# A two-layer hybrid network on one core: recurrent output projection as Strassen products that begin on sums already in PSUM, and a later start of the inner products in the second MLP

## The chip, the core and the metric

The kernel runs on one core of a Trainium2 chip. The metric is the device time of one execution in microseconds (us), from the first to the last instruction and what the device spends around them. Three runs of the kernel before gave 2066.32, 2066.69 and 2067.29 us; their median, 2066.69 us, is the time before.

## The reference

The sequence has 1024 tokens of 1024 features. There are two layers. Layer 0 mixes with sliding-window attention, layer 1 with a gated linear recurrence of eight heads; each is followed by an MLP with a squared ReLU and 4096 hidden features. All is fp32.

```python
def hgrn2_recurrence(h, lower_bound, w_in, g_norm, w_o):
    q, f, i, g = jnp.split(h @ w_in, 4, axis=-1)
    ...
    o = o.transpose(1, 0, 3, 2, 4).reshape(bsz, seq, HGRN_HEADS * HGRN_DV)
    o = rmsnorm(o, g_norm) * jax.nn.silu(g.astype(jnp.float32))
    return o.astype(h.dtype) @ w_o

def sqrelu_mlp(h, w_up, w_down):
    return jnp.square(jax.nn.relu(h @ w_up)) @ w_down

def reference(x, ...):
    for layer in range(DEPTH):
        h = rmsnorm(x, mix_norm[layer])
        y = sliding_window_attention(h, ...) if layer == 0 else hgrn2_recurrence(h, ...)
        x = x + y
        h = rmsnorm(x, mlp_norm[layer])
        x = x + sqrelu_mlp(h, mlp_w_up[layer], mlp_w_down[layer])
    return rmsnorm(x, final_norm)
```

The change touches the last line of `hgrn2_recurrence` (a product of 1024 x 1024 by 1024 x 1024, the "output projection" here), both MLPs, and the order at the very start.

## The kernel before

Every fp32 product is made of three TensorE products: both operands are split into a high and a low part (`split`, `weight_split`: one ScalarE cast, one VectorE subtraction for each 128x512 tile), and `mm3` adds high x high, high x low and low x high into one PSUM bank. A bank holds 128x512. There are eight: four with the tag `p`, four with the tag `q`.

Activations stand with features in partitions and are cut into two halves of 512 tokens, `hf` 0 and 1. A block product of two halves of features by two halves of tokens is done by Strassen's method in Winograd's form with seven products instead of eight. The products are numbered 1 to 7; 1, 6, 7, 4 share one running sum and 5, 3 (and 2) the others. Product 2 needs the upper features of half 0, product 1 the lower features of half 0, product 5, 6, 7, 3 need half 1, and product 4 needs all.

- **MLP, first projection** (`pair`, 16 pairs of output tiles a layer). Of each pair, products 1, 5, 6 and 7 are plain. From pair 2 on (`leaves`), products 2, 3 and 4 of two pairs together are done by a second, inner Strassen step (`inner_products`): 42 matmuls of 256 columns take the place of 24 matmuls of 512. Products 1 and 2 of pairs 0 and 1 are done ahead (`pair_first`), since they need only half 0.
- **MLP, second projection** (`down`). Passes over 16 contraction tiles: 1 with 5, then 6, 7, 2, 4, 3. Results of a pass are copied out of PSUM, added on VectorE to the others of their quarter, multiplied by the token scale (`scaled_sum`) and added to the residual.
- **Recurrent layer** (`hgrn`): eight heads, `gates` (four input projections) interleaved with `recurrence` of the head before. The gated outputs of each head are split and parked in DRAM (`put_by`), taken back at the end (`take_back`), and `hgrn_out` runs for half 0 and then half 1 as plain products: 8 output tiles x 8 contraction tiles x 3 = 192 matmuls a half. Between the halves `mlp_first` prepares the operands of half 0 for the MLP.
- **Start**: `scaled` splits the normalised input and then calls `token_rstd`, whose matmuls against a 128x1 column sum the squares over features. That matmul needs `sum_squares`, a chain of VectorE additions over all eight input tiles.

The order on every engine is set by the program itself: `Schedule.order` lists the operations with given durations, runs a list scheduler forward, ranks all but TensorE by latest start, and issues the best of four passes. A rank is the place of creation less `lead`. All tiles are recorded at one line, L429, so the rows of the trace are told apart by tile names: `p`, `q` banks; `wh`, `wl` high and low weights; `wr` raw weights; `a`, `t` activations; `m` short-lived sums; `d` DRAM.

Of the kernel before, what the change touches and what calls it, by code (L numbers as in the profile page):

```python
# [17 lines left out]
P = 128  # L18
# [125 lines left out]
FULL = {512: 227.3, 256: 119.8}  # L144
LEAD = 100
WARM = 11
ROWS = 16
EVACUATE = 100
HK = KT // 2


# [223 lines left out]
class Net:  # L375
# [203 lines left out]
    def spread(self, y, n=TH, r=None):  # L579

        r = (r or self.psum("q"))[:, :n]
        for j in range(n // P):
            self.mm(r[:, j * P : j * P + P], y[:, j : j + 1].to_broadcast([P, P]), self.ident, True, True, P, 4)
        return r
# [96 lines left out]
    def mlp_first(self, layer):  # L681
        self.layer, self.hid, self.y = layer, {}, {}
        yield from self.begin(2 + layer)
        self.weigh(0)

    def mlp_second(self):
        self.first = [self.pair_first(m) for m in range(2)]
        x = self.finish(2 + self.layer, keep=True)
        self.weigh(1)
        return x  # L690
# [128 lines left out]
    def pair(self, m, x, leaves):  # L819
# [6 lines left out]
        last, odd = m == half - 1, m % 2  # L826
        inner, four = [], ("12", "56", "73", "4")
        if leaves and odd:
            inner.append((2, (up[m - 1][:, TH:], 2), four, (1, 3, 5, 7)))
# [6 lines left out]
        w = self.strassen_weights(up[m], up[m + half], (2, 3, 4) if leaves else (1, 2), inner)  # L836

# [8 lines left out]
        def between(k):  # L846
            for z in now[k]:
                next(z)

        main, side = self.psum("q") if leaves else self.first[m], self.psum("q")  # L850
        now = [()] * 4
        if leaves:
            self.product(main, w[1], x[1], True)
            u1 = read(main)
            self.sums[2].append((m, u1))
            if odd:
                z2 = leaf(2, ((1, 2), (6, 5), (7, 3), (4,)))
                now = [[z2], [z2], [z2], [z2]]
            elif m > 3:
                z4, z3 = leaf(4, ((1, 2), (6, 5), (7, 3), (4,))), self.rest  # L860
                z3.send(w)
                now = [[z4, z3], [z4, z3], [z4], [z4]]
        between(0)
        self.product(side, w[5], x[5], True)
# [34 lines left out]
        if odd:  # L899
            for n, u in self.sums[2][-2:]:  # L900
                self.square_relu(n, 0, u, False)
        elif m > 3:
# [68 lines left out]
    def down(self, cut):  # L971
# [9 lines left out]
        def products(names, ps, ws, start, stop, tokens=slice(0, TH), ms=range(HK)):  # L981
            for p in ps:
                for name in names:
                    (wh, wl), (xh, xl) = ws[name, p]
                    for m in ms:
                        out = (main if name in (1, 6, 7, 4) else side)[m][:, tokens]
                        c = slice(m * P, m * P + P)
                        more = {"skip_group_check": True} if name in (6, 7, 4) or not start else {}
                        first = p == 0 and not more
# [468 lines left out]
    def recurrence(self, e, gates, totals, out):  # L1458
# [80 lines left out]
        for hf, (q, k) in enumerate(zip(qs, ks)):  # L1539
# [34 lines left out]
            self.stt(g, o, self.gain(5, e), g, ALU.mult, ALU.mult)  # L1574
            keep = e < KT - 1
# [30 lines left out]

    def hgrn_out(self, hf, y, total):
        r = self.t()
        self.copy(r, self.rstd(total, 0.25, 0.25))
        for m in range(KT):  # L1610
            w = self.blocks(self.weight(self.io["wg"][m]))
            x = self.t()
            self.dma(x, self.x[m][hf], 4 * P * TH)
            ps = self.psum()
            for kt in range(KT):
                self.mm3(ps, w[kt], y[kt], kt == 0, kt == KT - 1)
            z = self.t()
            self.tt("DVE", z, ps, r, ALU.mult)
            self.x[m][hf] = self.a()
            self.tt("any", self.x[m][hf], x, z, ALU.add)  # L1620

# [9 lines left out]
    def hgrn(self, layer):  # L1631
# [6 lines left out]
        self.spill(1)  # L1638
        ys, totals = [[], []], []
        before = iter(())  # L1640
        for e in range(KT):
            got = []
            interleave(self.gates(e, x, self.rs, r, got, [None] * 2 if e else begun), before, 14, 13)
            before = self.recurrence(e, got, totals, ys)
        run(before)
        for y in ys:
            y[:-1] = [self.take_back(kept) for kept in y[:-1]]
# [53 lines left out]
def layout(i):  # L1701
# [22 lines left out]
        "win": f(win.reshape(KT, P, 4, KT, P).transpose(2, 3, 1, 0, 4).reshape(4, KT, P, D)),  # L1724
        "wg": f(i["hgrn_w_o"][0].reshape(KT, P, KT, P).transpose(2, 1, 0, 3).reshape(KT, P, D)),
        "up": f(i["mlp_w_up"].reshape(2, KT, P, MT, P).transpose(0, 3, 2, 1, 4).reshape(2, MT, P, KT * P)),
# [39 lines left out]
```

## Time and profile before

| | us |
|---|---|
| median of three runs | 2066.69 |
| the profiled execution, its own time | 2068.61 |
| its span, first to last instruction | 2066.8 |
| TensorE busy | 2057.5 |
| VectorE busy | 1831.0 |
| ScalarE busy | 1203.6 |

The profiled execution took 1.8 us more than its span and 1.9 us more than the median of the runs without a profile. "Busy" of TensorE is the union of pipelined matmuls, each longer than the distance to the next, so its rate is read from the start of one stretch to the start of the next rather than from durations. By stage: attention up to about 300 us, its MLP to about 955, the recurrence to about 1366, its output projection to 1446, the second MLP to the end.

### The profile page before, as it was taken

The page shows a single profiled execution, that of the slowest core. Times are in us where ns is not written, and L with a number is a line of the kernel's source. Part 1 is how long each engine was busy: PE and PEld are TensorE (multiplying, and loading weights), DVE is VectorE, ACT ScalarE, POOL GpSimd, SP SyncE. Part 2 cuts the span into 40 slices and gives each one's busy share as a digit, 9 for nine tenths or more (in the row PEclk, how much of TensorE's full clock was granted, in tenths as well). Part 3 has the DMA queues.
Part 4 walks back from the last instruction along what each step waited for, and adds up shares of the span by engine and source line. Part 5 has one row for each costly group of instructions (what it writes and reads, how often), then busy time and mean ns, then how long its engine had stood idle before and what let it go on. Part 6 is the DMA issues. An engine that isn't in the chain of part 4 may idle for free.

```text
span 2066.8 us, 35765 instructions
## 1 busy us (share of the span) xinstructions
PE 2057.5 (100%) x12248; PEld 1747.5 (85%) x12248; DVE 1831.0 (89%) x3696; ACT 1203.6 (58%) x2468; POOL 54.7 (3%) x121
## 2 busy tenths in 40 slices
PE   9999999999999999999999999999999999999998
PEld 7878788898898888888888888888888888888888
DVE  8899889999899979889988888887999989986985
ACT  7577887644565444666555555555765456544473
POOL 3020000000000000000000000000000000000000
PEclk9999999999999999999999999999999999999999
DMA  6212477877679977541322222677887768986822
GB/s 220 82 49 80 128 237 257 278 244 237 225 253 304 332 222 257 196 138 67 113 102 95 96 103 103 219 239 226 273 275 256 230 229 265 311 315 210 270 67 82
DMA packets 225750, 407.43 MB, mean 197 GB/s; under 512 B 25232, under 2 KB 30352, under 8 KB 225568
## 3 DMA queue, kind: packets, MB, share of 16 engines
q1 hardware_dynamic: 225536, 405.12, 59.3%
q8 instruction: 96, 1.57, 0.3%
q14 instruction: 86, 0.70, 0.1%
q10 hardware_dynamic: 32, 0.03, 0.0%
HBM read 321.17 MB, written 83.89 MB: 196 GB/s over the span
## 4 chain that ended last, share of the span: by engine, by line
PE 96%; issue 1%; DVE 1%; ACT 0%; DMA 0%; POOL 0%; POOLq 0%; SPq 0%; DVEq 0%; ACTq 0%
PE p L429 51%; PE q L429 45%; DVE a L429 1%; DMA a<-in_x 0%; DVE m L429 0%; DVE t L429 0%; DVE wl L429 0%; ACT t L429 0%; ACT a L429 0%; DVE sm L429 0%; ACT wh L429 0%; POOL a L429 0%; POOLq L1740 0%; SPq L429 0%; ACT m L429 0%
## 5 line engine op out<-in xcount | busy, mean ns | idle before, releaser
L429 PE MATMUL p<-a,wh 128*128 128x512 f32 (+1 forms) x2880 | 805.0, 364 | 0.0
L429 PE MATMUL q<-a,wh 128*128 128x512 f32 x2112 | 652.9, 390 | 0.0
L429 PEld LDWEIGHTS p<-a,wh 128*128 128x128 f32 x2880 | 515.2, 189 | 84.4 <-issue 0.4
L429 PE MATMUL p<-a,wl 128*128 128x512 f32 (+1 forms) x1440 | 520.5, 362 | 0.0
L429 PEld LDWEIGHTS q<-a,wh 128*128 128x128 f32 x2112 | 389.7, 188 | 75.5
L429 PE MATMUL q<-a,wl 128*128 128x512 f32 x1056 | 410.2, 389 | 0.0
L429 ACT CAST wh<-m 128x512 fp32r<-128x512 f32 (+1 forms) x338 | 206.3, 613 | 262.1 <-PE q L429 172.2
L429 ACT CAST wh<-wr 128x512 fp32r<-128x512 f32 (+1 forms) x351 | 210.9, 603 | 227.8 <-PE p L429 165.2
L429 PEld LDWEIGHTS p<-a,wl 128*128 128x128 f32 x1440 | 271.6, 189 | 40.3 <-DVE wl L429 0.2
L429 DVE TENSOR_TENSOR wl<-m,wh 128x512 fp32r<-128x512 f32 (+1 forms) x338 | 226.8, 676 | 52.1 <-ACT wh L429 47.4
L429 DVE TENSOR_TENSOR wl<-wr,wh 128x512 fp32r<-128x512 f32 x352 | 233.2, 666 | 35.6 <-ACT wh L429 34.6
L429 PEld LDWEIGHTS q<-a,wl 128*128 128x128 f32 x1056 | 198.3, 188 | 41.9
L429 DVE TENSOR_TENSOR a<-t,a 128x512 fp32r<-128x512 f32 (+2 forms) x314 | 207.1, 679 | 14.5 <-PE q L429 8.8
L429 DVE TENSOR_TENSOR t<-t,t 128x512 f32<-128x512 f32 (+3 forms) x337 | 196.7, 602 | 13.8 <-ACT t L429 8.2
L429 ACT CAST a<-t 128x512 fp32r<-128x512 f32 (+1 forms) x234 | 139.1, 610 | 31.7 <-DMA t<-d 10.5
L429 ACT ACTIVATE t<-t 128x512 f32<-128x512 f32 x180 | 113.3, 632 | 73.4 <-DVE t L429 70.3
L429 ACT COPY t<-q 128x512 f32<-128x512 f32 (+2 forms) x201 | 111.3, 558 | 28.8 <-PE q L429 23.3
L429 PE MATMUL p<-wh,a 128*128 128x512 f32 x384 | 125.7, 397 | 0.0
L429 DVE TENSOR_TENSOR m<-wr,wr 128x512 f32<-128x512 f32 (+1 forms) x188 | 121.6, 647 | 2.9 <-DMA wr<-in_down 1.6
L429 DVE TENSOR_TENSOR t<-t,p 128x256 f32<-128x256 f32 x294 | 119.7, 416 | 3.7 <-PE p L429 1.8
L429 PEld LDWEIGHTS q<-t,t 128*64 128x64 f32 (+1 forms) x2160 | 96.0, 144 | 12.1 <-issue 8.1
L429 PE MATMUL q<-t,t 128*64 128x32 f32 (+2 forms) x2160 | 104.7, 229 | 0.0
(129 smaller groups left out, 2327.4 us busy)
## 6 DMA issues: line engine op xcount, KB each, us to landing
t<-d SPq DMA_DIRECT2D x548, 256.0 KB, 4.2
d<-t SPq DMA_DIRECT2D x244, 256.0 KB, 3.2
wr<-in_down SPq DMA_DIRECT2D x224, 256.0 KB, 4.2
wr<-in_up SPq DMA_DIRECT2D x178, 256.0 KB, 3.8
wr<-in_win SPq DMA_DIRECT2D x68, 256.0 KB, 2.8
a<-d SPq DMA_DIRECT2D x60, 256.0 KB, 3.7
wr<-in_wqkv SPq DMA_DIRECT2D x48, 256.0 KB, 2.9
d<-a SPq DMA_DIRECT2D x48, 256.0 KB, 3.9
```

Source lines behind the costliest of these rows:

```text
L429: fn(*[place(a) for a in args], **{k: place(v) for k, v in kw.items()})
```

## The change

1. The output projection becomes seven Strassen products (`hgrn_out`, in the order 1, 5, 2, 6, 3, 7, 4). `recurrence` no longer splits the gated output as it is, but hands it to `out_operands`, which forms the differences that the seven products need and parks them in DRAM. `out_weight` forms the sums of weights, from another layout of the weights in DRAM.
2. Product 2 has its own banks (`side`, tag `q`). So that it adds onto product 1, a matmul first writes each of these banks (its result is not used), ScalarE copies product 1's sum over it, and product 2 accumulates. Products 3 and 4 begin in the same way on sums that ScalarE or VectorE wrote into `side`.
3. `hgrn_out` is now one generator: after product 2 and after product 4 it yields, and four steps of `mlp_first` follow.
4. In the second MLP, inner products start at pair 4 instead of pair 2 (`INNER = 2, 4`); pairs 2 and 3 are done with all seven plain products. The token sums of squares (`weigh`) of that layer move behind pair 1.
5. In both second projections, two quarters are copied into `side` ahead of passes 2 and 3, which then accumulate onto them; the additions afterwards go away.
6. At the start, `token_rstd` of half 0 gets a later rank (`BEHIND`).

```diff
+BEHIND = 120
+INNER = 2, 4
+FIRSTS = 2, 2
+ORDER, AHEAD, HELD = (1, 5, 2, 6, 3, 7, 4), 2, (3, 7, 4)
...
     def scaled(self, which, hf):
-        return h, self.token_rstd(self.sum_squares([self.x[kt][hf] for kt in range(KT)]))
+        total = self.sum_squares([self.x[kt][hf] for kt in range(KT)])
+        self.s.lead = 0 if hf else -BEHIND
+        r = self.token_rstd(total)
+        self.s.lead = 0
+        return h, r
...
     def pair(self, m, x, leaves):
-        elif leaves and m > 3:
+        elif leaves and m > INNER[self.layer] + 1:
...
+        elif not begun:
+            own = self.psum()
+            self.product(main, w[1], x[1], True)
+            u1 = read(main)
+            self.product(own, w[2], x[2], True)
+            self.tt("DVE", u1, own, u1, ALU.add)
+            self.square_relu(m, 0, u1, False)
...
     def mlp(self, cut):
-            if m == 2:
+            if m == INNER[self.layer]:
...
-            self.pair(m, x, m > 1)
+            self.pair(m, x, m >= INNER[self.layer])
+            if self.layer and m == 1:
+                self.weigh(0)
+                self.weigh(1)
...
     def down(self, cut):
-        for i in range(2):
-            for m in range(HK):
-                z = residual(m + (1 - i) * HK, 1)
-                scaled_sum(1, z, y[1 - i, 1, m])
-                self.x[m + (1 - i) * HK][1] = z
+        for m in range(HK):
+            z = residual(m + HK, 1)
+            scaled_sum(1, z, y[1, 1, m])
+            self.x[m + HK][1] = z
+        for m in range(HK):
+            self.copy(side[m], y[0, 0, m], psum=False)
         run_pass((2,))
-        parts = [self.t() for _ in range(HK)]
         for m in range(HK):
-            self.copy(parts[m], side[m])
+            z = residual(m, 0)
+            scaled_sum(0, z, side[m])
+            self.x[m][0] = z
         for m in range(HK):
-            self.tt("DVE", y[0, 0, m], parts[m], y[0, 0, m], ALU.add)
-            z = residual(m, 0)
-            scaled_sum(0, z, y[0, 0, m])
-            self.x[m][0] = z
+            self.copy(side[m], y[0, 1, m], psum=False)
+            self.x[m][1] = residual(m, 1)
         run_pass((4,))
...
     def recurrence(self, e, gates, totals, out):
-            y = self.split(g, self.t if keep else None)
-            out[hf].append(self.put_by(y) if keep else y)
+            self.out_operands(e, hf, g, out)
...
+    def out_operands(self, e, hf, g, x):
+        def put(name, z):
+            y = self.split(z, self.a if last else self.t)
+            x[name].append(y if last else self.put_by(y))
+        if hf == 0:
+            put(1 if e < HK else 2, g)
+            self.beside = g
+        elif e < HK:
+            self.tt("any", self.beside, g, self.beside, ALU.subtract)
+            put(5, self.beside)
+            self.later.append((self.keep(self.beside), self.keep(g)))
+        else:
+            t, q = (self.back(z) for z in self.later[p])
+            self.tt("any", t, g, t, ALU.subtract)
+            put(6, t)
...
+    def hgrn_out(self, x, totals):
...
+        products(1, main, True)
+        for m in range(HK):
+            self.copy(p1[m], main[m])
+        products(5, main, False)
+        for m in range(HK):
+            w, z = ready[2, 0]
+            self.mm(side[m], w[0][:, :P], z[0], True, True)
+            self.copy(side[m], p1[m], psum=False)
+            self.tt("DVE", p5[m], main[m], p1[m], ALU.subtract)
+        products(2, side, False)
+        for m in range(HK):
+            scaled_sum(0, m, side[m])
+        yield
+        products(6, main, False)
+        for m in range(HK):
+            self.copy(side[m], main[m])
+        products(3, side, False)
+        for m in range(HK):
+            scaled_sum(1, m, side[m])
+        products(7, main, False)
+        for m in range(HK):
+            self.tt("DVE", side[m], main[m], p5[m], ALU.subtract)
+            scaled_sum(1, m + HK, main[m])
+        products(4, side, False)
+        for m in range(HK):
+            scaled_sum(0, m + HK, side[m])
+        yield
...
     def hgrn(self, layer):
-        self.hgrn_out(0, ys[0], totals[0])
-        run(self.mlp_first(layer))
-        self.hgrn_out(1, ys[1], totals[1])
+        first = self.mlp_first(layer)
+        for _ in self.hgrn_out(y, totals):
+            for _ in range(HK):
+                next(first)
+        run(first)
```

Here `products(name, bank, start)` runs the 4 x 4 x 3 matmuls of one product, and takes operands back two steps ahead.

How the instructions move is shown at three places. The first is TensorE at the start, in the first of three column groups of the query, key and value projection; `q_400` (before) and `q_466` (the change) are the banks of the sums of squares, `t_234` the sum, `wh` and `wl` the weights of one contraction tile. Before:

```order
L429 MATMUL p_263<-wl_310,a_300 128x512
L429 MATMUL p_263<-wh_294,a_319 128x512
L429 MATMUL p_272<-wh_294,a_300 128x512
L429 MATMUL q_400<-c_69,t_234 128x1 x4
L429 MATMUL p_272<-wl_310,a_300 128x512
L429 MATMUL p_272<-wh_294,a_319 128x512
```

With the change:

```order
L433 MATMUL p_253<-wl_360,a_353 128x512
L433 MATMUL q_466<-c_69,t_234 128x1
L433 MATMUL p_253<-wh_339,a_382 128x512
L433 MATMUL q_466<-c_69,t_234 128x1
L433 MATMUL p_263<-wh_339,a_353 128x512
L433 MATMUL q_466<-c_69,t_234 128x1
L433 MATMUL p_263<-wl_360,a_353 128x512
L433 MATMUL q_466<-c_69,t_234 128x1
```

The four column matmuls stood together behind the 46th matmul of 512 columns, in the fourth contraction tile; now they stand one by one behind the 65th and later, in the sixth.

The second place is TensorE in the output projection, where product 5 ends (`p_16317` is the last of its four banks) and product 2 begins on `q_16893`, `q_16897`, `q_16899`, `q_16902`:

```order
L433 MATMUL p_16317<-a_16263,wl_16593 128x512
L433 MATMUL q_16893<-a_16492,wh_16450 128x512
L433 MATMUL q_16897<-a_16492,wh_16450 128x512
L433 MATMUL q_16899<-a_16492,wh_16450 128x512
L433 MATMUL q_16902<-a_16492,wh_16450 128x512
L433 MATMUL p_16277<-a_16509,wh_16891 128x512
L433 MATMUL p_16277<-a_16518,wh_16891 128x512
L433 MATMUL q_16893<-a_16492,wh_16450 128x512
L433 MATMUL q_16893<-a_16529,wh_16450 128x512
```

The four matmuls that only mark the banks come right behind product 5; two matmuls of product 6 (`p_16277`) stand between them and the first that accumulates. ScalarE has the four copies in one row after the cast of product 6's weight:

```order
L433 CAST wh_16891<-a_16182 128x512
L433 COPY q_16893<-a_16462 128x512
L433 COPY q_16897<-a_16522 128x512
L433 COPY q_16899<-a_16544 128x512
L433 COPY q_16902<-a_16549 128x512
L433 CAST a_16923<-a_16192 128x512
```

Nothing of this stood in the program before. The third place is TensorE where product 4, the last, ends on `q_16902` and the MLP's `pair_first` begins (`q_17489` product 1 of pair 0, `p_17522` its product 2, `q_17527` product 1 of pair 1):

```order
L433 MATMUL q_16902<-a_17008,a_17253 128x512
L433 MATMUL q_16902<-a_17079,a_17253 128x512
L433 MATMUL q_16902<-a_17008,a_17282 128x512
L433 MATMUL q_17489<-a_17057,wh_17023 128x512
L433 MATMUL q_17489<-a_17088,wh_17023 128x512
L433 MATMUL q_17489<-a_17057,wl_17032 128x512
```

After seven more rows of `q_17489`:

```order
L433 MATMUL q_17489<-a_17138,wh_17023 128x512
L433 MATMUL q_17489<-a_17105,wl_17032 128x512
L433 MATMUL p_17522<-a_17511,wh_17044 128x512
L433 MATMUL q_17527<-a_17057,wh_17120 128x512
L433 MATMUL q_17527<-a_17088,wh_17120 128x512
```

Before, the whole of half 0's operands was ready when the projection of half 1 ended. Now `a_17511`, the first operand of product 2, comes from product 4's banks, and twelve matmuls on `q_17489` stand between.

More of the change, by code (lines that the diff above doesn't have):

```diff
@@ L1605, in double @@
         return at + n, new, *out
[L1607 to L1620, printed above, removed]
+    def out_operands(self, e, hf, g, x):
+        p, last = e % HK, e == KT - 1
+        def put(name, z):
[12 more added lines that the diff above has]
+            put(6, t)
+            self.tt("any", self.beside, self.beside, t, ALU.subtract)
+            put(4, self.beside)
+            self.tt("any", q, g, q, ALU.subtract)
+            put(7, q)
+            put(3, g)
@@ new lines, in hgrn_out, with operand, products, scaled_sum @@
+    def hgrn_out(self, x, totals):
+        kept, y, r = {}, {}, [self.a() for _ in range(NH)]
+        order = [(name, p) for name in ORDER for p in range(HK)]
+        ready = {}
+        def operand(name, p):
+            w = self.out_weight(name, p, kept)
+            z = x[name][p]
+            return w, self.take_back(z) if isinstance(z, list) else z
+        def products(name, bank, start, apart=False):
+            todo = order.index((name, 0))
+            for p in range(HK):
+                for q in order[: todo + p + 1 + AHEAD]:
+                    if q not in ready:
+                        ready[q] = operand(*q)
+            got = [ready[name, p] for p in range(HK)]
+            turns = [(p, m) for p in range(HK) for m in range(HK)]
+            more = {} if start else {"skip_group_check": True}
+            for p, m in sorted(turns, key=lambda k: k[1]) if apart else turns:
+                c, (w, z) = slice(m * P, m * P + P), got[p]
+                self.mm3(bank[m], (w[0][:, c], w[1][:, c]), z, start and p == 0, p == HK - 1, **more)
+        def scaled_sum(hf, m, z):
+            u, out = self.t(tag="m"), self.a()
+            self.tt("DVE", u, z, r[hf], ALU.mult)
+            self.dma(out, self.x[m][hf], 4 * P * TH)
+            self.tt("any", out, u, out, ALU.add)
+            self.x[m][hf] = out
+        for hf in range(NH):
+            self.copy(r[hf], self.rstd(totals[hf], 0.25, 0.25))
+        main, side = [self.psum() for _ in range(HK)], [self.psum("q") for _ in range(HK)]
+        p1, p5 = ([self.a() for _ in range(HK)] for _ in range(2))
+        products(1, main, True)
[25 more added lines that the diff above has]
+        yield
@@ L1638, in hgrn @@
         self.spill(1)
-        ys, totals = [[], []], []
+        y, totals, self.later = {k: [] for k in range(1, 8)}, [], []
         before = iter(())
```

70 lines of the change are left out of this document (49 added, 21 removed).

## Prediction, made before the changed kernel ran

> **What bounds the kernel now.** I read the page first, for the share of each engine and the chain of work that ended last.
>
> ```profile
> span 2066.8 us, 35765 instructions
> PE 2057.5 (100%) x12248; PEld 1747.5 (85%) x12248; DVE 1831.0 (89%) x3696; ACT 1203.6 (58%) x2468; POOL 54.7 (3%) x121
> PE 96%; issue 1%; DVE 1%; ACT 0%; DMA 0%; POOL 0%; POOLq 0%; SPq 0%; DVEq 0%; ACTq 0%
> ```
>
> TensorE is in the chain for 96% of the span. A busy TensorE can still be a waiting one, so the second view is the list of what TensorE waited for, in the whole execution:
>
> ```profile
> PE q L429 <- DVE sm L429: 1.4, 1, 1.4
> PE p L429 <- DVE t L429: 1.0, 1, 1.0
> PE q L429 <- DVE t L429: 1.0, 1, 1.0
> PE q L429 <- DVE m L429: 0.3, 1, 0.3
> ```
>
> Four waits, 3.7 us of 2066.8. So a matmul taken away is worth its full distance to the next, and work given to or taken from the other engines is worth nothing as long as it makes TensorE wait nowhere. That distance comes from long unbroken stretches in the chain of waits (start, length, what):
>
> ```profile
> 790.44 43.52 PE p L429 x192
> 1404.70 41.62 PE p L429 x183
> 1736.05 8.63 PE p L429 x72
> ```
>
> The first two are matmuls of 512 columns, the second of them the output projection itself: 43.52 / 192 = 0.2267 us, 41.62 / 183 = 0.2274. The third is of 256 columns (inner products): 8.63 / 72 = 0.1199 us. A half-width matmul costs 53% of a whole one.
>
> **The output projection.** Before, 2 halves x 8 x 8 x 3 = 384 matmuls of 512 columns. Now seven products of 4 x 4 x 3 = 336, and four that mark banks: 340. That is 44 fewer: 44 x 0.2267 = 9.97 us less.
>
> **Pairs 2 and 3 of the second MLP.** Three inner products go, each 42 half-width matmuls in the place of 24 whole ones. 72 x 0.2267 = 16.32 us come, 126 x 0.1199 = 15.11 us go: 1.21 us more. TensorE's two orders differ by the same net counts, +28 of 512 and -126 of 256 columns; nothing else on it changes in number.
>
> **The start.** The third wait of the list stands here; in TensorE's timeline (start, length in us, what, how many):
>
> ```profile
> 16.45 0.61 PE L429 MATMUL p<-wh,a 128*128 128x512 f32 x2
> 18.09 1.05 PE L429 MATMUL q<-c,t 128*128 128x1 f32 x8 [1.03 <-DVE t L429]
> 19.00 0.48 PE L429 MATMUL p<-wl,a 128*128 128x512 f32 x1
> 20.22 1.05 PE L429 MATMUL p<-wh,a 128*128 128x512 f32 x2
> 21.08 0.63 PE L429 MATMUL p<-wl,a 128*128 128x512 f32 x1
> ```
>
> The second of the two matmuls at 16.45 is through at 16.45 + 2 x 0.2267 = 16.90, and the next of 512 columns starts at 19.00. Of these 2.10 us the column matmuls take 19.00 - 18.09 = 0.91, which I leave in; 1.19 us are the wait. Then two matmuls take 21.08 - 20.22 = 0.86 us, twice as long as above. The stretches show why (last but two: clock granted):
>
> ```profile
> 17.00:19.00 2.00, 0.97 (x9) 0.91 (x9) 2.00 (x6) 2.00 (x4) 0.00 (x0) 1.00 0.51 173
> 19.80:23.20 3.40, 3.40 (x10) 2.63 (x9) 3.37 (x19) 0.67 (x2) 0.00 (x0) 0.51 0.74 232
> 23.20:31.80 8.60, 8.60 (x39) 7.12 (x38) 5.76 (x21) 7.00 (x12) 0.00 (x0) 1.00 0.84 250
> ```
>
> TensorE's clock was halved for 3.4 us right behind the wait, so some 1.6 us more are lost (half of 3.4, less the edges). The sum of squares is ready here:
>
> ```profile
> 17.34 0.69 DVE L429 TENSOR_TENSOR t<-t,t 128x512 f32<-128x512 f32 x1
> ```
>
> This addition ends at 18.03. In the new order the column matmuls come behind 65 matmuls instead of 46, at about 16.90 + 19 x 0.2267 = 21.2 us. VectorE's order puts more of the weights' low parts ahead of the sum; even with two more such operations of 0.69 us it is done at 19.4. So I take the wait as gone, and the half clock with it: 1.19 + 1.6 = 2.8 us less. Late next would be the scale of the first results: from the sum at 21.2 to the scale, VectorE and ScalarE have until block 0 of the group ends, about 16.90 + 41 x 0.2267 + 0.9 = 27.1 us. Bounds: 0 (the wait comes back there) and 2.8.
>
> The Trainium skill, "TensorE: Matmul & The Clock Gate", section "HAM oscillation — how this bites in real kernels", asks for no idle gap above about 3.4 us, one whole idle window; a gap of 1.2 us, or 2.1 with the column matmuls in it, should not halve the clock. The trace's gap did come before a halved stretch, of the length that the page gives. By the page the halved stretch has another cause and stays, and this term would be 1.2 instead of 2.8; that is a rival below.
>
> **Marked banks.** The copies into PSUM have no row in the trace. The nearest rows are a copy out of PSUM and a cast between SBUF tiles, on ScalarE, an operation of VectorE that reads PSUM, and the gain multiplication:
>
> ```profile
> L429 ACT COPY t<-p 128x512 f32<-128x512 f32 x72 | 41.8, 583 | 1.6 <-PE p L429 1.5
> L429 ACT CAST a<-t 128x512 fp32r<-128x512 f32 x226 | 136.3, 618 | 31.7 <-DMA t<-d 10.5 <-DVE t L429 9.7 <-PE q L429 8.3
> L429 DVE TENSOR_TENSOR t<-p,t 128x512 f32<-128x512 f32 x68 | 47.0, 692 | 28.8 <-PE p L429 27.1 <-ACT t L429 1.5
> L429 ACT ACTIVATE t<-a,c 128x512 f32<-128x512 f32 x48 | 34.2, 721 | 16.6 <-DVE a L429 16.5
> ```
>
> At product 2 the first bank's seed has five matmuls to hide behind (three markers, two of product 6): 5 x 0.2267 = 1.13 us, against 0.16 (a matmul's drain, 0.39 long at a distance of 0.23) + 0.62 = 0.8. Each later bank has three more matmuls, 0.68 us, for one more copy of 0.62. So it just fits: 0. If product 2 waited for all four copies it would be 0.16 + 4 x 0.62 - 1.13 = 1.5 us. At products 3 and 4 the copies of a bank can begin while the other three finish, nine matmuls or 2.04 us: 0 there, at most 0.6 each. Bounds 0 to 2.7; I take 0.4, near the lower end, because each bank is handed on by itself in the orders.
>
> **Into the MLP.** Behind product 4's first bank nine matmuls of the others and twelve of `q_17489` cover the first operand of `p_17522`: 21 x 0.2267 = 4.8 us. What it needs: drain 0.16, three multiplications that stand ahead and one addition on VectorE, 4 x 0.69 = 2.8, gain 0.72, cast 0.62: 4.3. No wait. VectorE is what could give out there:
>
> ```profile
> 1340.00:1446.00 106.00, 106.00 (x699) 89.56 (x698) 84.91 (x167) 60.25 (x116) 0.61 (x2) 1.00 0.72 235
> 1457.00:1511.00 54.00, 54.00 (x265) 45.56 (x264) 53.18 (x108) 36.70 (x68) 0.00 (x0) 1.00 0.81 268
> 700.00:710.00 10.00, 10.00 (x45) 8.28 (x45) 10.00 (x18) 4.23 (x8) 0.00 (x0) 1.00 1.02 370
> 1830.00:1840.00 10.00, 10.00 (x46) 8.28 (x45) 9.52 (x16) 4.23 (x9) 0.00 (x0) 1.00 1.05 404
> ```
>
> In the second row, the MLP's first 54 us, VectorE was busy 53.18 and TensorE still never waited. Counted in the orders from the first read of the projection's last banks to pair 2's first weight, VectorE had 60 operations of 512 and 17 of 256 columns for 208 matmuls; now it has 80 and 2 for 242. With 0.69 and 0.42 us each: 48.5 against 47.2 us of TensorE before, 56.0 against 54.9 now, a ratio of 1.03 before and 1.02 now (the operations overlap a little). Cost 0.
>
> **Second projections.** Eight copies into PSUM a layer on ScalarE, twelve VectorE operations fewer. Each copy has the whole pass before it, 192 matmuls or 43.5 us, as cover. 0; without cover 1.5 us each time, four times.
>
> **Sum.** -9.97 + 1.21 - 2.79 + 0.4 = -11.15 us on the span of 2066.8. The profiled execution itself took 2068.61, 1.9 above the median of the runs; the difference is taken off the median: 2066.69 - 11.15 = **2055.5 us**.
>
> **Rivals.**
>
> *The half clock stays* (0.13). The gap goes, the slow stretch is caused by something else at the start: 1.6 back, 2057.1. For it: the stretch begins 0.8 us after matmuls have resumed. Against it: it begins within a microsecond of the only wait that TensorE has in this stage.
>
> *The start's wait comes back at the evacuation* (0.09). Scale ready too late, all 2.8 lost again: 2058.3. For it: all four `p` banks are in use there, and the next group cannot begin without one. Against it: several us in hand, as worked out.
>
> *DMA becomes the bound in the output projection* (0.08), the way it turns slower. Operands of all seven products now come back from DRAM; by SP's orders, from the first such load to the last before product 4 ends, 113 transfers of 256 KB stand for 340 x 0.2267 = 77.1 us of matmuls and about 10 of the last head's recurrence. At 235 GB/s, the rate of the stage before (first row above), a transfer is 1.12 us and 113 take 126: 39 us of wait, 2094. At 370, the rate of a saturated stretch (share 1.02), 0.71 us and 80: no wait. The bound decides from 0.77 us a transfer (341 GB/s) on, and the gain is gone at 0.87 (302 GB/s). At 300 GB/s with no load sent ahead: 113 x 0.874 = 98.8, less 87, 2055.5 + 11.8 = 2067.3; at 285 GB/s, 2072.4, slower. Against it: 370 and 404 GB/s were reached without a wait, 235 was all that was asked for, and loads stand well ahead of their use.
>
> *The seams cost what the upper ends say* (0.08): +2.3 at the marked banks and a second halved stretch of 1.7: 2059.5.
>
> The forecast itself has 0.62, its own range 2053.5 to 2057.
>
> **How the numbers follow.** Two tenths of a percent, about 4.1 us, is what can be told from no change. Faster by more means below 2062.6: the forecast and the rivals but for most of DMA, 0.92. Within: part of DMA, 0.05. Slower, above 2070.8: 0.03. The range leaves out the worst of the seams and DMA: 2053 to 2060.
>
> **What would show it.** The matmul counts, +28 and -126, at 0.227 and 0.120 us. TensorE's list of waits without the one on VectorE near 18 us, and a clock of 1.00 from 17 to 32 us; if the second fails and the first holds, the halved stretch has another cause. No idle of TensorE with ScalarE as releaser between products of the projection; a wait there on a load, with a DMA share near 1, would be the DMA rival. VectorE near full in the MLP's first 55 us, with TensorE still not waiting. If TensorE's waits add up to more than 8 us, the argument as a whole is wrong: then the order, and not the number of matmuls, sets the time.

## The result, and the profile after

| | before | after |
|---|---|---|
| median, us | 2066.78 (2066.32 to 2069.16) | 2060.96 (2058.98 to 2064.92) |
| ratio, 95% interval | | 0.9972 (0.9964 to 0.9980) |
| span of the profiled execution | 2066.8 | 2063.1 |
| own time of the profiled execution | 2068.61 | 2064.92 |

The change gains 5.8 us, where 11.2 were forecast; the time lies above the range, which ended at 2060. The profiled execution of after is the slowest of its ten, 4.0 us above their median. One execution of r3 (7245.88 us) and one of r6 (2113.10 us) below were slow ones, which stand in the medians but in no ratio, interval or spread. The page of after, the same rows as were shown of before:

```profile
span 2063.1 us, 35536 instructions
PE 2049.8 (99%) x12150; PEld 1737.7 (84%) x12150; DVE 1830.7 (89%) x3675; ACT 1226.0 (59%) x2508; POOL 58.5 (3%) x121
PE 86%; DVE 8%; DMA 3%; issue 3%; ACT 1%; POOL 0%; POOLq 0%; SPq 0%; DVEq 0%; ACTq 0%
```

The number of matmuls fell by 98 (12248 to 12150), as +28 and -126 make it. But TensorE's share of the chain that ended last fell from 96 to 86%: VectorE and transfers took part of it. What TensorE waited for (us in total, times, longest):

```profile
PE q L433 <- ACT a L433: 2.7, 1, 2.7
PE p L433 <- DVE t L433: 1.6, 2, 1.0
PE q L433 <- DVE sm L433: 1.4, 1, 1.4
PE q L433 <- ACT m L433: 0.5, 1, 0.5
PE q L433 <- DVE t L433: 0.4, 1, 0.4
PE q L433 <- ACT t L433: 0.4, 1, 0.4
PE q L433 <- DVE a L433: 0.2, 1, 0.2
PE q L433 <- issue: 0.2, 1, 0.2
```

These are 7.4 us, against 3.7 before. The longest stands in layer 0, in front of the MLP's second projection; all engines there (start, length, what, idle before and releaser):

```profile
697.34 0.62 ACT L433 CAST a<-m 128x512 fp32r<-128x512 f32 x1 [4.07 <-DVE m L433]
697.83 0.68 DVE L433 TENSOR_TENSOR a<-t,a 128x512 f32<-128x512 f32 x1
...
699.75 0.62 ACT L433 CAST a<-a 128x512 fp32r<-128x512 f32 x1 [1.27 <-DVE a L433]
...
700.91 0.73 PE L433 MATMUL q<-a,wh 128*128 128x512 f32 x2 [2.68 <-ACT a L433]
```

ScalarE waits for VectorE, and TensorE for ScalarE; VectorE itself stands, from 690 us on, in a chain of operations with no gap. Ahead of that, between 640 and 680 us, it had waited 2.9 us for loads; these come back with r1 below. The window 650 to 700 us of before shows how little reserve there is (window and length, busy of TensorE, weight loads, VectorE, ScalarE, GpSimd, then clock, DMA share, GB/s):

```profile
650.00:700.00 50.00, 50.00 (x222) 41.42 (x221) 48.66 (x81) 25.80 (x46) 0.00 (x0) 1.00 0.91 312
```

VectorE was busy 48.66 of 50 us there and TensorE still did not wait. The code of this stage did not change in the part ahead of the wait.

To compare traces I add up, from the starts of neighbouring matmuls, what exceeds 0.2267 us (512 columns) or 0.1199 us (256): called "lost" below. Excesses of about 0.1 us at the ends of bursts, which every trace has, are left out; at the start and on the way into the projection narrower matmuls count too. The table has it for the start (first 60 us), layer 0's MLP, the way into and through the output projection, and layer 1's MLP up to the final norm.

| trace | start | MLP 0 | projection | MLP 1 |
|---|---|---|---|---|
| before | 6.38 | 0 | 0 | 0 |
| after | 5.71 | 3.36 | 0.67 | 1.22 |

So 5.25 us were lost in stages where before lost nothing, and only 0.7 was won at the start. Two places stand in no column: attention, which lost 2.2 us in before, 3.1 in after and in r1, and 2.3 to 3.5 in the others; and the end of layer 0's MLP at 943 to 945 us, where r5, r10, r12, r14 and r16 below lose 0.8 to 1.2.

### The profile page after: what moved, and what is told of

It is laid out like the page before. It is cut to its first block, busy times and chain, and to the rows that moved or that the text cites. A ratio compares the mean times of both kernels' runs of the same rounds, so it can differ in the third digit from the quotient of the medians.

```text
span 2063.1 us, 35536 instructions
## 1 busy us (share of the span) xinstructions
PE 2049.8 (99%) x12150; PEld 1737.7 (84%) x12150; DVE 1830.7 (89%) x3675; ACT 1226.0 (59%) x2508; POOL 58.5 (3%) x121
## 4 chain that ended last, share of the span: by engine, by line
PE 86%; DVE 8%; DMA 3%; issue 3%; ACT 1%; POOL 0%; POOLq 0%; SPq 0%; DVEq 0%; ACTq 0%
PE p L433 43%; PE q L433 42%; DVE t L433 3%; DVE a L433 2%; DVE wl L433 1%; DVE m L433 1%; DMA wr<-in_down 1%; DMA d<-t 1%; DMA t<-d 0%; DMA wr<-in_wg 0%; ACT t L433 0%; ACT wh L433 0%; DVE sm L433 0%; ACT a L433 0%; DMA wr<-in_up 0%
## 5 line engine op out<-in xcount | busy, mean ns | idle before, releaser
L433 PE MATMUL p<-a,wh 128*128 128x512 f32 (+1 forms) x2680 | 752.1, 364 | 0.5 <-DVE t L433 0.5
L433 PE MATMUL q<-a,wh 128*128 128x512 f32 x2180 | 674.1, 391 | 3.3 <-ACT a L433 2.7
L433 PEld LDWEIGHTS p<-a,wh 128*128 128x128 f32 x2680 | 479.2, 189 | 79.2 <-DVE t L433 0.7
L433 PE MATMUL p<-a,wl 128*128 128x512 f32 (+1 forms) x1340 | 484.7, 362 | 0.0
L433 ACT CAST wh<-wr 128x512 fp32r<-128x512 f32 (+1 forms) x323 | 194.5, 604 | 195.8 <-PE p L433 128.8
L433 PEld LDWEIGHTS p<-a,wl 128*128 128x128 f32 x1340 | 252.7, 189 | 37.2 <-DVE wl L433 0.4
L433 DVE TENSOR_TENSOR wl<-wr,wh 128x512 fp32r<-128x512 f32 (+1 forms) x324 | 214.4, 665 | 32.4 <-ACT wh L433 30.2
L433 ACT COPY t<-q 128x512 f32<-128x512 f32 (+1 forms) x199 | 109.9, 558 | 26.1 <-PE q L433 11.5
L433 DVE TENSOR_TENSOR a<-a,a 128x512 fp32r<-128x512 f32 (+2 forms) x151 | 100.8, 679 | 17.8 <-PE p L433 9.6
L433 ACT CAST a<-a 128x512 fp32r<-128x512 f32 x136 | 82.8, 619 | 52.2 <-DVE a L433 45.4
```

Source lines behind the costliest of these rows:

```text
L433: fn(*[place(a) for a in args], **{k: place(v) for k, v in kw.items()})
```

## The experiments

"Lost" is for the profiled execution of each, the ratio for its runs against runs of before beside them. The four groups had medians of before of 2066.8, 2067.1, 2066.9 and 2067.4 us, so medians of different groups compare to about 0.6 us.

**Again, and one part at a time.** r1 is the changed kernel as it is. r2 to r4 are the kernel before with one part of the change:

```diff
 r2: hgrn_out by Strassen, and nothing else
+        for _ in self.hgrn_out(y, totals):
 r3: inner products from pair 4 on in layer 1, sums of squares later
+INNER = 2, 4
+            if self.layer and m == 1:
+                self.weigh(0)
+                self.weigh(1)
 r4: the norm's sum of squares later
+        self.s.lead = 0 if hf else -BEHIND
```

> The changed kernel once more, as it is, for a second trace. Theory P (the planned order is late): the waits of TensorE that the first trace has sit in the order, above all the 2.7 us at 697.8 us in front of the first operand of layer 0's second projection; they come again at the same places, within 0.5 us each, and about 2061 us. Rival R (chance of the execution): transfers and clock differ from one execution to the next; the wait at 697.8 is under 0.5 us here, others stand elsewhere, and the time follows the sum of what there is. Of the half-rate stretch near the start (6.7 to 9.8 us): under P at the same place, under R somewhere else or not there.

> The kernel before with the output projection by Strassen alone (44 matmuls of 512 columns fewer, with the marked banks). My sum: -9.97 + 0.4, a ratio of 0.9954, about 2057.2 us. Theory P (new waits come with any new plan): 2 to 4 us less of a gain, 2059 to 2061, with waits of TensorE outside the projection. Rival S (the projection's own seams cost more than I took): waits between 1360 and 1450 us that add up to over 2 us, the rest of the program as before.

> The kernel before with only the second MLP's change: inner products from pair 4 on, sums of squares behind the first two pairs. My sum: +1.21 us, 2068.0 us. Theory P: waits are added in layer 1 or anywhere, +2 us or more beyond it, 2070. Rival: the order that comes out has less for VectorE to do at the start of the second MLP, so none beyond +1.2.

> The kernel before with only the norm's sum of squares put 120 operations later (no matmul more or less). My sum: -2.8 us, 2064.0 us, with the wait at 18.1 us and the half-rate stretch from 19.8 to 23.2 both gone. Rival H (the half-rate stretch is not caused by the wait): the wait goes and the half-rate stretch stays or lies elsewhere, -1.2 us, 2065.6. Theory P: the new plan puts waits elsewhere, and the time is 2066 or more.

| | median | ratio | start | MLP 0 | projection | MLP 1 |
|---|---|---|---|---|---|---|
| r1 | 2061.58 | 0.9975 (0.9965 to 0.9985) | 4.08 | 1.46 | 1.03 | 1.17 |
| r2 | 2065.93 | 0.9993 (0.9985 to 1.0002) | 5.81 | 0.79 | 1.10 | 6.06 |
| r3 | 2067.70 | 1.0002 (0.9993 to 1.0011) | 2.91 | 0 | 0 | 0 |
| r4 | 2065.18 | 0.9991 (0.9982 to 1.0000) | 4.20 | 0 | 0 | 0 |

r1 is between its two theories. Most places come again: 0.3 us near 396, at 582 (1.19, in the first trace 0.23), ahead of the projection (1.03, 0.67), at 1729 (1.17, 0.68). But at 697 us nothing is lost this time, where the first trace lost 2.84. The order sets where TensorE can be caught; the execution sets how much.

What the execution sets is how late a transfer lands. Two of the places in r1, each with the wait of ScalarE for a store or a load and the wait of TensorE behind it:

```profile
582.70 0.59 ACT L433 COPY t<-q 128x512 f32<-128x512 f32 x1 [1.39 <-DMA d<-t]
...
583.34 0.73 PE L433 MATMUL q<-a,wh 128*128 128x512 f32 x2 [1.03 <-ACT t L433]
```

```profile
1727.50 0.62 ACT L433 CAST a<-t 128x512 fp32r<-128x512 f32 x1 [2.97 <-DMA t<-d]
...
1730.76 0.51 PE L433 MATMUL p<-a,wh 128*128 128x256 f32 x2 [1.01 <-DVE t L433]
```

The same waits in other traces, beside what TensorE lost there:

| place | trace | waited for the transfer | TensorE lost |
|---|---|---|---|
| 582 us, ScalarE, a store | after | 0.42 | 0.23 |
| | r11 | 0.81 | 0.61 |
| | r8 | 1.28 | 1.08 |
| | r1 | 1.39 | 1.19 |
| 1730 us, ScalarE, a load | after | 2.47 | 0.68 |
| | r1 | 2.97 | 1.17 |

At 582 us the loss is the wait less 0.2 in all four, at 1730 us the wait less 1.8 in both: the order leaves that much slack, and what exceeds it reaches TensorE. At 697 us it is less exact. VectorE's waits for loads of the second projection's weights between 560 and 701 us, in after and then in r1:

```profile
DVE m L433 <- DMA wr<-in_down: 2.9, 4, 0.9
```

```profile
DVE m L433 <- DMA wr<-in_down: 0.9, 2, 0.5
```

They are 2.0 us longer in after, in the stage with 1.3 us of reserve, and TensorE lost 2.84 there against 0.

r2 is the surprise. With 44 matmuls fewer, 9.97 us, it gains 0.9. The same window in r2 and in after, behind the projection:

```profile
1452.00:1457.40 5.40, 2.74 (x10) 1.64 (x10) 5.40 (x10) 5.40 (x12) 0.00 (x0) 1.00 0.54 203
1457.40:1460.80 3.40, 3.40 (x9) 2.59 (x9) 3.40 (x7) 2.14 (x4) 0.00 (x0) 0.52 0.82 269
```

```profile
1452.00:1457.40 5.40, 5.40 (x25) 4.46 (x25) 5.40 (x10) 4.88 (x9) 0.00 (x0) 1.00 0.91 329
1457.40:1460.80 3.40, 3.40 (x17) 2.82 (x16) 3.40 (x6) 3.40 (x8) 0.00 (x0) 1.00 0.44 162
```

In r2 VectorE and ScalarE are both full (5.40 of 5.40) and TensorE gets through 10 matmuls instead of 25; then the clock is halved for 3.4 us. The parts are not additive: r2 to r4 gain 0.9, lose 0.9 and gain 1.6, together 1.6, and the whole gains 5.8. Each of the three intervals reaches 1, so single gains are hardly clear of noise; that the seam makes the difference is borne out by r11 below. What the pairs' edit does beside its matmuls is to free that seam. Whether the later inner products or the later sums of squares do it, no run separates.

r3 also explains the start. It has before's order there, but not its wait. ScalarE's second gained operand, in before and in r3, and r3's first column matmuls:

```profile
7.93 0.72 ACT L429 ACTIVATE a<-a,c 128x512 fp32r<-128x512 f32 x1 [1.20 <-DMA a<-in_x]
```

```profile
6.73 0.73 ACT L433 ACTIVATE a<-a,c 128x512 fp32r<-128x512 f32 x1
...
16.89 1.05 PE L433 MATMUL q<-c,t 128*128 128x1 f32 x8
```

In before's profiled execution one load of the input came 1.20 us late. The last addition of the sum of squares, on VectorE, started 1.19 us later than in r3 (17.34 against 16.15), and the wait of 1.19 us at 18 us is that load. In r3 it came in time: no wait, and no halved stretch behind. It is not a single accident: in r9, the kernel before in another order, the same load came 1.18 us late, with a wait of 1.07 and a halved stretch behind it.

**Other orders of the same work.** r5 and r6 only tell the planner other transfer times, r7 moves the projection's scale, r8 undoes the second projection's part:

```diff
 r5
-LOAD, STORE = 3000.0, 2000.0
+LOAD, STORE = 5000.0, 5000.0
 r6
-LOAD, STORE = 3000.0, 2000.0
+LOAD, STORE = 2900.0, 2000.0
 r7
-        for hf in range(NH):
-            self.copy(r[hf], self.rstd(totals[hf], 0.25, 0.25))
...
         products(1, main, True)
+        for hf in range(NH):
+            self.copy(r[hf], self.rstd(totals[hf], 0.25, 0.25))
 r8
-        for m in range(HK):
-            self.copy(side[m], y[0, 0, m], psum=False)
...
+            self.tt("DVE", y[0, 0, m], parts[m], y[0, 0, m], ALU.add)
```

> The changed kernel with the planner told that a load and a store take 5.0 us each, where it had 3.0 and 2.0 (in the trace of the changed kernel the median of a t<-d load is 4.2, nine tenths are under 5.6). Nothing else changes; no instruction more or less. Theory L (the plan counts on transfers that are faster than the chip's, so operands and buffers come late wherever the plan has no slack): the waits of TensorE in the MLPs (2.4 to 4.2 us in the two traces) fall under 1 us in all, about 2058 us, and the runs spread less. Theory P (any plan is as good or bad by luck): between 2058 and 2064, with waits at other places. Rival (earlier loads hold buffers longer): slower than 2062.

> The changed kernel with the planner's load time at 2.9 us in the place of 3.0: another order of the same instructions, with no reason to be better or worse. Theory P (luck of the order): its waits stand elsewhere and the time lies 1 to 3 us from 2061, on either side. Theory L: the waits stay of the same sum, 2 to 5 us, 2060 to 2062. If it comes back with the same time within 0.5 us, the order's luck counts for little and the losses belong to the change.

> The changed kernel with the scale of the output projection (column sums and spread on TensorE) put behind product 1 in the place of ahead of it. The two traces show TensorE waiting 0.7 and 1.0 us for VectorE in front of these, at 1363 to 1368 us. If that wait comes from where the sums stand: it goes, -0.7 to -1.0 us, about 2060. Rival: the wait only moves to product 1's first operands or to the copy behind it, no gain; or the plan changes elsewhere and the time moves by up to 3 us either way.

> The changed kernel with the second projection of both MLPs as it was before (two quarters are added up outside PSUM again; as many matmuls, twelve operations of VectorE more a layer, eight of ScalarE fewer). My term was 0: 2061 us. Rival (the quarters completed in PSUM take VectorE work off a saturated stretch, which is where the wait at 697.8 us stood): slower here, waits of 1 to 3 us more around 690 to 900 us, 2062 to 2064. Rival (the copies into PSUM cost): faster, 2058 to 2060.

| | median | ratio | start | MLP 0 | projection | MLP 1 |
|---|---|---|---|---|---|---|
| r5 | 2058.53 | 0.9961 (0.9949 to 0.9974) | 3.03 | 0 | 2.44 | 0 |
| r6 | 2059.82 | 0.9965 (0.9953 to 0.9977) | 2.81 | 0.62 | 0.34 | 0.58 |
| r7 | 2057.68 | 0.9958 (0.9944 to 0.9972) | 5.57 | 0 | 0.75 | 0 |
| r8 | 2059.33 | 0.9968 (0.9956 to 0.9981) | 5.97 | 1.08 | 1.59 | 0.61 |

r7 was to give 0.7 to 1.0 us and came out 3.3 below after: the losses in both MLPs, which its edit does not touch, are gone. r6 has no reason to be better at all, and its trace lost 1.5 us in the three stages instead of 5.25 and 3.66. r8 came out lower than after, but its interval covers after's ratio, so no difference is shown and my 0 for that part is not contradicted.

**The kernel before under the same edits, the seam, and both edits.** r9 is before with r6's line, r10 before with r5's; r11 is after without r3's part; r12 has r5's and r7's edits.

```diff
 r11
-            if m == INNER[self.layer]:
+            if m == 2:
...
-            if self.layer and m == 1:
-                self.weigh(0)
-                self.weigh(1)
 r12: r7's lines, and
+LOAD, STORE = 5000.0, 5000.0
```

> The kernel before (not the changed one) with the planner's load time at 2.9 us in the place of 3.0: the same instructions in another order. Theory P (the order before happened to be one without waits, and any other order of it has 1 to 5 us of them; the changed kernel lost that when it was planned anew): slower, 2068 to 2071, with waits of TensorE in the MLPs or ahead of the output projection. Rival C (the waits belong to the changed parts): no new waits, 2066 to 2067.5.

> The kernel before with the planner's load and store time at 5.0 us. Theory L (transfers slower than planned make the waits, and the kernel before has hardly any left): no change, 2066 to 2067.5. Theory P: another draw of the order, 2066 to 2071, with waits anywhere.

> The changed kernel without the second MLP's part (its inner products from pair 2 on again, its sums of squares ahead of the pairs). By the matmul counts alone: -1.21, 2059.8. Theory S (with the Strassen projection ahead of it, VectorE cannot carry the sums of squares, the weights and the first operands at once, as in the run with the projection alone, which lost 5.7 us between 1451 and 1468 us): those waits come back, with a halved clock behind them, +4.5, about 2065.5. Theory P: the loss at that seam was of one order, and here it is under 2 us.

> The changed kernel with the scale's sums behind product 1 and the planner's load and store time at 5.0 us, the two edits that were faster. If the waits each took away were different ones: 2056 to 2057. If each was only another draw of the order (theory P): 2056.5 to 2060, with other waits. Rival: 5.0 us of planned load holds buffers longer and the projection's end gets waits with a halved clock behind them as in the run with 5.0 us alone, 2058 to 2060.

| | median | ratio | start | MLP 0 | projection | MLP 1 |
|---|---|---|---|---|---|---|
| r9 | 2067.56 | 1.0004 (0.9995 to 1.0012) | 5.70 | 0 | 0 | 0.85 |
| r10 | 2066.18 | 0.9997 (0.9988 to 1.0005) | 2.94 | 0 | 0 | 0.21 |
| r11 | 2065.20 | 0.9991 (0.9983 to 1.0000) | 5.45 | 1.19 | 0.76 | 6.41 |
| r12 | 2058.09 | 0.9958 (0.9945 to 0.9972) | 2.80 | 0 | 0.37 | 0 |

r11 confirms theory S: without the pairs' edit the seam loses its 5 to 6 us again. The matmul counts alone had it 1.2 us faster than after; it is 4.2 slower.

r10 and r12 are the pair of traces with the least lost: before and after, both planned with 5.0 us, both with a start of 2.8 to 2.9, both with 0.84 at 943 us and hardly a loss elsewhere. I picked this pair after the results, and r12 has r7's lines besides. The spans, r10 and then r12:

```profile
span 2064.0 us, 35621 instructions
```

```profile
span 2056.1 us, 35474 instructions
```

That is 7.9 us, and 8.1 between the medians. Without r7's lines, r10 to r5 (both planned with 5.0 us) is 7.7 between the medians, and r9 to r6 (both with the nudge) 7.7. My terms without the start are -9.97 + 1.21 + 0.4 = -8.36. The pairs hold the start's edit as well, which no run separates in these orders. What r12's TensorE still waits for:

```profile
PE q L433 <- DVE sm L433: 1.4, 1, 1.4
PE p L433 <- DVE t L433: 1.0, 1, 1.0
PE p L433 <- ACT t L433: 0.7, 1, 0.7
...
```

r9 came out 0.7 us above and r10 0.7 us below their own runs of before (2066.90); both intervals hold 1. r9 lies between the ranges of its two theories, and its trace lost 0.85 us in layer 1; the kernel before has more reserve than I expected under theory P.

**Luck or transfer times.** Still open was whether the waits come from planned transfers (3.0 and 2.0 us) that are shorter than the chip's. The median from issue to landing, in the trace of after:

```profile
t<-d SPq DMA_DIRECT2D x526, 256.0 KB, 4.2
d<-t SPq DMA_DIRECT2D x270, 256.0 KB, 3.1
```

r13 is r7 with the nudge, r14 is r5 with it; r15 and r16 are after with one time changed:

```diff
 r13: r7's lines, and
+LOAD, STORE = 2900.0, 2000.0
 r14
+LOAD, STORE = 5200.0, 5000.0
 r15
+LOAD, STORE = 3000.0, 5000.0
 r16
+LOAD, STORE = 5000.0, 2000.0
```

> The changed kernel with the scale's sums behind product 1 and the planner's load time at 2.9 us: the r7 kernel in another order, still planned with transfers faster than the chip's. Theory P or L (r7's lack of waits in the MLPs was a lucky draw): waits of 1 to 3 us there again, 2059 to 2061. Rival (moving the sums is what took them away): none, 2057.5 to 2058.5.

> The changed kernel with planned loads of 5.2 and stores of 5.0 us: the r5 kernel in another order, planned with transfers about as slow as the chip's. Theory L (honest transfer times keep the slack where it is needed): no wait of TensorE over 0.3 us in the MLPs, 2057.5 to 2059. Theory P: as with 2.9 in the place of 3.0, waits of 1 to 3 us somewhere, 2059 to 2061.

> The changed kernel with planned stores of 5.0 us, loads left at 3.0. The wait at 582 us hung on a store (a buffer to be read out to memory before it is written again), those at 697 and 1729 us on loads. Theory L: the first goes, waits on loads of 1 to 3 us stay, 2059 to 2061. Theory P: any place, 2058 to 2062.

> The changed kernel with planned loads of 5.0 us, stores left at 2.0. Theory L: the waits on loads go, one on a store of up to 1.2 us may stay, 2058 to 2060. Theory P: any place, 2058 to 2062.

| | median | ratio | start | MLP 0 | projection | MLP 1 |
|---|---|---|---|---|---|---|
| r13 | 2056.42 | 0.9948 (0.9935 to 0.9960) | 4.15 | 0.31 | 0.85 | 0 |
| r14 | 2058.59 | 0.9957 (0.9945 to 0.9970) | 4.14 | 0 | 0.41 | 0.70 |
| r15 | 2057.42 | 0.9955 (0.9941 to 0.9968) | 3.01 | 0 | 0 | 0.65 |
| r16 | 2059.39 | 0.9961 (0.9949 to 0.9974) | 3.57 | 0.62 | 0.57 | 0 |

The fastest of all, r13, was planned with the short times and came out below every range that I gave, and so did r15. So theory L, which explains single waits as r1 showed, does not explain the medians. r13's waits:

```profile
PE q L433 <- DVE sm L433: 1.4, 1, 1.4
PE p L433 <- DVE t L433: 1.2, 2, 1.0
PE q L433 <- DVE t L433: 0.6, 1, 0.6
PE q L433 <- ACT m L433: 0.2, 1, 0.2
```

3.4 us in all, where before had 3.7. The instructions of the change, in eight other orders (r5, r6, r7, r12 to r16), have medians from 2056.4 to 2059.8. The order that after has, at 2061.0 and in r1 at 2061.6, is the slowest of the nine. All five runs of r12 (2057.85 to 2058.31), of r13 (2055.95 to 2057.64) and of r14 (2058.34 to 2058.96) lie below the fastest of after's eighteen (2058.98).

What the long times did is narrow the runs. With loads and stores at 5.0 us or more, r5, r12 and r14 spread over 1.4, 0.5 and 0.6 us, and r10 over 1.0 in eleven runs; with one or both of the times short it is 5.9 for after, 3.3 for r1, 1.7 to 4.1 for r6 to r8, r13, r15 and r16, and 4.3 for r9 and r11. A likely reason, not tested by itself: from 60 to 2050 us VectorE waits for transfers 0 to 0.4 us in all in the traces of r5, r10, r12 and r14, 1.6 in r16 and 4.2 to 14.8 in the others. It does not decide alone: r13 has the 14.8, and its five runs spread over 1.7.

r13 beats both kernels: 2056.42 us.

## Why the prediction was wrong, step by step

- **TensorE bounds it, and a matmul is worth its distance**: right. After has stretches such as this (start, length, what), 43.52 / 192 = 0.2267 us:

```profile
792.80 43.52 PE p L433 x192
```

- **Output projection, pairs, marked banks (-9.97 + 1.21 + 0.4)**: borne out where the orders lose alike, 8.36 against 7.7 to 8.1 in three pairs of medians. Were the start's edit worth its 1.6 us in them too, 6.1 to 6.5 would be left for these terms; that is open. No bank's marking shows as a wait. It was a sum for two orders with equal losses.
- **Start (-2.79)**: the mechanism held, but the size was taken from one execution. Wait and halved stretch were there in before's profiled execution and came of a late load. I made the sum against that execution and then took it off the median, although the execution stood 1.9 us above the median: that gap was a sign that part of the term was not in the median. By itself the edit is worth 1.6 us (r4, 0 to 3.7 by its interval, which does not shut 2.79 out). After has no wait there and a clock of 1.00, but its load was only 0.35 us late. That the new place of the sums removes the wait is shown by r15, where the load came 1.52 us late, the clock stayed at 1.00 and nothing on TensorE waited. The window in after, then the load and the window in r15:

```profile
17.00:32.00 15.00, 15.00 (x71) 12.53 (x71) 11.81 (x53) 9.71 (x19) 0.00 (x0) 1.00 0.78 231
```

```profile
8.09 0.72 ACT L433 ACTIVATE a<-a,c 128x512 fp32r<-128x512 f32 x1 [1.52 <-DMA a<-in_x]
```

```profile
17.00:32.00 15.00, 15.00 (x71) 12.54 (x71) 14.58 (x66) 12.15 (x23) 0.00 (x0) 1.00 0.83 271
```

- **"Work given to the other engines is worth nothing as long as it makes TensorE wait nowhere"**: the step that failed. I checked the condition only at the seams of the change. The planner puts the whole program in a new order, and layer 0's MLP, whose VectorE had 1.3 us of reserve in 50, got 1.5 to 3.4 us of losses; with the way into the projection and layer 1, 3.7 (r1) and 5.25. The 1.9 us of the base and r1's 3.7 make about the 5.5 by which the forecast missed; it is a rough account, for attention lost another 0.8 that is not in it. That these losses belong to this order is shown by r12 to r15, which have 0 to 0.3 in layer 0's MLP (r12 and r14 lose 0.8 and 1.2 at its very end); that late transfers fill them is shown at 582 and 1730 us. Why the planner chose this order is not shown.
- **Into the MLP (0)**: right for the whole change, but for a reason that I did not give. I counted the pairs' edit as a cost of 1.21; r2 and r11 show that the projection without it loses 5 to 6 us there.
- **Second projections (0)**: no difference shown (r8).
- **Rivals**: the halved stretch goes with its wait. Before and r9 have both, r2, r3 and r10, which have the sums near where before has them, neither. The seams' upper ends gave 2059.5, the nearest time, but by luck: no wait stood at the banks. DMA was no bound: in the projection its share was 0.80 at 271 GB/s, and TensorE had 0.4 us of idle, on VectorE:

```profile
1365.00:1446.00 81.00, 80.61 (x426) 67.64 (x423) 74.05 (x135) 50.95 (x91) 0.00 (x0) 1.00 0.80 271
```

None of the four named the order itself.
- **The bound of 8 us of waits**: 7.4 and 6.1 stayed under it, and yet the order cost a third of the gain. It should have been set against the 3.7 of before.

## What to carry to other kernels

When a planner orders the whole program, an edit is also a new draw of the order. Here the draw of the change is the slowest of nine, 2.4 to 3.1 us above the middle one, so a gain of that size is to be read over a few nudged orders of both kernels, not from one pair. A wait in a single trace goes into the sum against the median only as far as that trace stands where the median does. Cost the parts of a change together as well: one that adds matmuls can be what lets another one pay.

## What was not expected of the hardware

**The clock halves after little, and not after much.** r5 lost 0.41 us at 1374.5 and had sixteen column matmuls around it; then the clock was halved (the last but two is the clock granted):

```profile
1372.80:1376.20 3.40, 3.16 (x24) 2.60 (x22) 3.13 (x6) 2.87 (x5) 0.00 (x0) 1.00 0.00 0
1376.20:1379.70 3.50, 3.50 (x10) 2.79 (x10) 3.29 (x14) 3.03 (x7) 0.00 (x0) 0.51 0.25 80
```

In after the wait of 2.7 us at 697.8 was followed by a full clock (TensorE alone):

```profile
697.80:700.90 3.10, 0.43 (x2) 1.00 0.86 293
700.90:704.30 3.40, 3.39 (x15) 1.00 0.92 306
```

The Trainium skill, "TensorE: Matmul & The Clock Gate", section "HAM oscillation — how this bites in real kernels", asks for no idle gap above about 3.4 us. The second case agrees. The first, the wait of 1.03 us in before, and r2, whose longest wait ahead of its halved stretch was 2.23 us, do not: the gap alone does not decide. Column matmuls stand beside it in r5 and in before, but not in r2; what does decide is not shown.

**The start differs from trace to trace by up to 3.2 us.** By the spacing of matmuls, the first ones at the full rate start at 4.5 to 10.7 us in the eighteen traces (10.2 in after, 7.0 in r1, the same kernel). In the thirteen that have the column matmuls behind the 65th, the start's loss lies between 2.80 and 5.97. The Trainium skill, "TensorE: Matmul & The Clock Gate", section "What's actually happening", has the window over which TensorE's activity is watched free-running, so that the transition falls differently from run to run, by 500 ns either way. That it differs agrees; here it differs by 6 us. The granted clock does not show this stretch. In after it reads 1.00 while ten matmuls take 3.15 us, because the clock's records in that trace begin at 10.18 us:

```profile
6.65:9.80 3.15, 3.15 (x10) 2.47 (x10) 2.67 (x5) 2.79 (x6) 0.61 (x5) 1.00 1.02 381
```

So half rates at the start are read from the distance between matmuls, not from the clock.
